# The second column pair of w_down's first half: eleven seven-product blocks laid between the second up stage's projections

## The chip, the cores and the metric

The kernel runs on one core of a Trainium2 chip. The metric is the device time of one execution in microseconds, and the profile is that of one execution. PE is the engine that multiplies matrices, DVE, ACT and POOL are the three engines that work on vectors, and SP issues the loads and stores. What PE writes goes to one of eight PSUM banks (128 partitions by 512 floats), and DVE or ACT reads it from there.

## The reference

One decoder layer in float32 on 256 positions with 2048 channels: an input projection, two kinds of attention, an output projection, and then the channel mixer, with which this change is concerned:

```python
h = rmsnorm(x, pre_ffn_g[l])
u = causal_dwconv(h @ w_up[l], conv_w[l], conv_b[l])          # 256 x 11264
gate, val = jnp.split(u, 2, axis=-1)
y = (jax.nn.gelu(gate, approximate=True) * val) @ w_down[l]   # 5632 -> 2048
x = x + rmsnorm(y, post_ffn_g[l])
```

## The kernel before

A float32 operand is split into a high and a low part (`fp32r`): ACT casts the high part, DVE subtracts it for the low part, and a product is then three matmuls (high by high, high by low, low by high). Each weight unit of 128x1024 therefore costs one load by SP, one cast on ACT and one subtraction on DVE before PE may use it. The loads go to a ring of five `raw` tiles, the parts to a ring of five `wpair` tiles.

The channel mixer runs in two halves of 2816 hidden channels. The **up stage** of a half has eleven steps `g`. A step projects 256 gate channels and then 256 value channels (`proj_S`: 96 matmuls of 128x256 into one PSUM bank, from four weight units). After each of the two, DVE reads the bank into a tile `u` (`rows_of`, below called the evacuation), ACT and DVE run the convolution on it, ACT applies the gelu to the gate channels, and DVE multiplies. The result is split into the tiles `G` (two per step), which are the stationary operands of the down stage. `LONG` and `LATE` are orders in which the high and low parts of the four units are used: `LONG` begins with the high part of the first unit, `LATE` with its low part.

The **down stage** of a half multiplies `G` by 22 blocks of rows of w_down, in two column pairs, `n = 0` and `n = 2` (each is two blocks of 512 columns). Two row blocks are handled together as a 2x2 block product. A *four* takes one column block the plain way, so a pair of columns costs 8 products; a *seven* does the pair with 7 products (Strassen's scheme in Winograd's form). One product is three matmuls of 128x512, so a seven has 21 where two fours have 24. A seven needs sums of `G` tiles (POOL adds them, ACT and DVE split them into `sums` or `more`) and sums of weight blocks. The weight sums are made on DVE when the block is used (four subtractions of 128x512, `L1105`), or were made earlier, in the up stage: `stage` loads a block into `staged`, subtracts on DVE (`L928`, four of 128x256, twice a block), and stores it to DRAM for later (`STORED`). `SEVENS` says how many sevens a column pair of a half has and after which pair of fours each stands. In half 0 both column pairs have six sevens and five pairs of fours. After the last seven `fold` adds four banks into `y_sb`, and `down` adds the others.

PE's order is the program's order. ACT's, DVE's, POOL's and SP's are set by a scheduler before the run; each engine then works strictly in its order, and an instruction that waits holds up everything behind it on its engine.

Of the kernel before, what the change touches and what calls it, by code (L numbers as in the profile page):

```python
# [17 lines left out]
P = 128  # L18
# [9 lines left out]
SEVENS = (((0, 0, 1, 1, 2, 2), (0, 0, 1, 1, 2, 2)), ((0, 0, 1, 1, 2), (0, 1, 2)))  # L28
STORED = (((0, 0, 1), (0, 0, 3), (0, 0, 5), (0, 2, 1), (0, 2, 3), (0, 2, 5), (1, 0, 1)), ((1, 0, 3), (1, 2, 0), (1, 2, 1), (1, 2, 2)))
# [5 lines left out]
def hybrid_layer(ctx: ExitStack, tc: tile.TileContext, x, pre_mix_g, w_in, b_forget, sinks,  # L35
# [817 lines left out]
    with tc.tile_pool(name="ffn", bufs=1) as fp:  # L853
# [123 lines left out]
        gbf = None  # L977
        for half in range(2):
            G = [fp.tile([P, 512], F32R, tag="G", bufs=FHALF, name=f"G{j}")[:, 0:512]
                 for j in range(FHALF)]  # L980
            most = max(len(at) for at in SEVENS[half])
            least = min(len(at) for at in SEVENS[half])
            sums = []

            def sums_at(u):
                w, at = 384 if u < least else 512, 768 * min(u, least) + 1024 * max(u - least, 0)
                if not u:
                    sums.append(main.tile([P, 4096], F32R, tag="x", name="sums"))
                if at + 2 * w <= 4096:
                    x = sums[0][:, at:at + 2 * w]  # L990
                else:
                    x = fp.tile([P, UNIT], F32R, tag="gb1", name="more")[:, 0:2 * w]
                sums.append((x[:, :w], x[:, w:]))
                return w, *sums[-1]

            for g in range(FHALF // 2):
                c0 = (half * (FHALF // 2) + g) * 256
                alt = (g + half) % 2
                if half == 0 and g == 0:
                    bg = first_gate()  # L1000
                    order.__exit__(None, None, None)
                    bv = [bank(), bank()]
                    proj_T(w_up, DFF + c0, bv, LONG)
                else:
                    bg = bank("att") if alt else bank()
                    proj_S(w_up, c0, bg, LATE if g + half == 1 else LONG)
                gates = []
                yy = fp.tile([P, 4, 256], F32, tag="yy", bufs=2, name="yy")
                for m, u in enumerate(rows_of(bg)):
# [7 lines left out]
                for m, u in enumerate(rows_of(bv)):  # L1017
# [3 lines left out]
                if g < most:  # L1021
# [6 lines left out]
                    if g < least:  # L1028
                        s1 = a21
# [4 lines left out]
                for m, y in enumerate(ys):  # L1034
                    gt = G[g * 2 + m]
                    split(gt[:, 0:256], gt[:, 256:512], y)
                if g < most:
                    w, *parts = sums_at(g)
                    split(*parts, s[:, :w])
                if not g:  # L1040
                    if half:
                        room = lambda: fp.tile([P, 4, 256], F32, tag="gb0", name="staged")
                    else:
                        four_of = main.tile([P, 4, 4, 256], F32, tag="y", name="staged")
                        rooms = [four_of[:, i] for i in range(4)]
                        room = lambda: rooms.append(rooms[0]) or rooms.pop(0)
# [10 lines left out]
            gains, downs = [], []  # L1057

            def down(t, n, b, gain=None):
                ys = y_sb[:, t, n * 512:(n + 1) * 512]  # L1060
                downs.append(dve.tensor_tensor(ys, b, ys, op=ALU.add))
                if half:
                    act.activation(junk, ys, AF.Square, scale=D ** -0.5,
                                   accum_out=ysq[t][:, n:n + 1])
                    (gain or pool.tensor_tensor)(
                        ys, ys, gbf[n // 2][:, n % 2 * 512:(n % 2 + 1) * 512], op=ALU.mult)

            LAST = FHALF // 2 - HOLD

            def products(b, held, hi, lo, opened, closes=False):  # L1070
                for i, (x, r) in enumerate(((held[0], hi), (held[0], lo), (held[1], hi))):
                    pe.matmul(b, x, r, start=b not in opened and not i,  # L1072
                              stop=closes and i == 2)
                opened.append(b)

            def parts_of(k, t):
                return G[k][:, t * P:(t + 1) * P], G[k][:, 256 + t * P:256 + (t + 1) * P]

            def split_into(dst, src, n):
                hi, lo = (x[:, :n * 512] for x in dst)  # L1080
                split(hi, lo, src[:, :n * 512])
                return [(hi[:, i:i + 512], lo[:, i:i + 512]) for i in range(0, n * 512, 512)]

            def seven(n, u, last, banks, opened):

                b, e, g, a, c, d, f = banks
                k = half * FHALF + u * 2
                t = in_dram.get((half, n, u))
                if t is None:
                    top, low = [w_load(w_rows(w_down, k + i, 1, n * 512, 1024), 1, 1024, raw=x)[0]  # L1090
                                for i, x in enumerate((None, fp.tile(
                                    [P, UNIT], F32, tag="yy", bufs=2, name="low")))]
                else:
                    top = w_load(w_rows(w_down, k, 1, n * 512, 512), 1, 512)[0]
                    low = w_load(w_rows(w_down, k + 1, 1, n * 512, 1024), 1, 1024)[0]
                s2, s3, s4, s1 = [
                    [x[:, i * P:i * P + P] for x in sums[1 + u]] if i < 3 or u >= least
                    else parts_of(u * 2, 1) for i in range(4)]
                (w11,) = split_into(w_parts(UNIT, held=False), top, 1)
                w21, w22 = split_into(w_parts(UNIT, held=False), low, 2)  # L1100
                if t is None:
                    b11, b12, b21, b22 = (x[:, i:i + 512] for x in (top, low) for i in (0, 512))
                    for y, p, q in ((b11, b12, b11), (b12, b22, b12), (b22, b22, b11),
                                    (b21, b21, b22)):
                        made = dve.tensor_tensor(y, p, q, op=ALU.subtract)  # L1105
                        if n and not u and y is b11:
                            tc.add_manual_dep(
                                made.ins, downs[-1].ins.name,
                                mybir.DependencyInfo(mybir.DependencyClass.NoSync,
# [203 lines left out]
```

## Time and profile before

| | us |
|---|---|
| median of 3 runs | 1053.0 (1052.75 to 1053.56) |
| the profiled execution: its own time | 1053.05 |
| the profiled execution: its span | 1051.2 |

Of the span PE is busy 99%, DVE 80%, ACT 60% and POOL 16%. The up stage of half 0 runs from 359.62 us (its second step) to 577.24, the down stage of half 0 to 688.80, the up stage of half 1 to 928.20, and the last down stage to the end. PE waits for nothing between 359 and 1046 us; it is the bound there. Where a table or a list below has a matmul group with 3 of its instructions missing, and a gap of that length, the records are missing and not the work.

### The profile page before, as it was taken

What the parts mean: (1) busy time and instruction counts of PE and PEld (TensorE: products, weight loads), DVE (VectorE), ACT (ScalarE), POOL (GpSimd) and SP (SyncE); (2) the same over time, 40 slices, a digit from 0 to 9 for tenths busy, and PEclk for the clock granted to TensorE, in tenths of its full rate; (3) what the DMA queues carried; (4) which work ended last, traced back from release to release, by engine and by line L of the source; (5) the groups of instructions that cost most, each with busy time, mean ns of one, the idle gap of its engine ahead of it and who ended that gap; (6) DMA issues with size and microseconds to landing.
All of it is one profiled execution on the core that took longest, in us unless ns stands there. A gap on an engine that the chain in (4) does not pass through costs nothing.

```text
span 1051.2 us, 19023 instructions
## 1 busy us (share of the span) xinstructions
PE 1040.2 (99%) x7240; PEld 958.1 (91%) x7240; DVE 836.9 (80%) x1364; ACT 627.7 (60%) x1026; POOL 168.0 (16%) x211
## 2 busy tenths in 40 slices
PE   9999999999999999999999999999999999999997
PEld 7899988888888999999999888899999999988886
DVE  5999877887477898888877988967788777789783
ACT  6777757667556755555555655645565555566561
POOL 3253245441122210100000000000111000000023
PEclk9999999999999999999999999999999999999998
DMA  8645556555874878988875886777677776767792
GB/s 292 199 128 169 182 157 213 164 179 172 292 252 148 257 253 289 290 271 268 285 233 168 263 270 222 241 238 239 222 228 249 227 241 221 235 210 257 243 320 104
DMA packets 187335, 238.98 MB, mean 227 GB/s; under 512 B 8268, under 2 KB 155116, under 8 KB 186348
## 3 DMA queue, kind: packets, MB, share of 16 engines
q1 hardware_dynamic: 186924, 237.30, 69.4%
q8 instruction: 57, 0.93, 0.3%
q10 hardware_dynamic: 320, 0.47, 0.1%
q14 instruction: 34, 0.28, 0.1%
HBM read 221.86 MB, written 15.75 MB: 226 GB/s over the span
## 4 chain that ended last, share of the span: by engine, by line
PE 90%; DVE 4%; ACT 2%; POOL 1%; DMA 1%; issue 1%; DVEq 0%; SPq 0%; ACTq 0%; POOLq 0%
PE bank_att L300 23%; PE bank_acc L300 21%; PE bank_acc L1072 15%; PE bank_acc L317 12%; PE bank_acc L263 5%; PE bank_att L1072 5%; PE bank_acc L270 3%; DVE wpair L122 1%; DMA raw<-in_w_in_dram 1%; PE bank_att L317 1%; POOL scr L450 1%; PE bank_att L518 1%; PE bank_att L483 1%; PE bank_att L527 1%; ACT p L501 1%
## 5 line engine op out<-in xcount | busy, mean ns | idle before, releaser
L122 DVE TENSOR_TENSOR wpair<-raw,wpair 128x1024 fp32r<-128x1024 f32 (+3 forms) x317 | 383.6, 1225 | 115.5 <-ACT wpair L119 114.5
L119 ACT CAST wpair<-raw 128x1024 fp32r<-128x1024 f32 (+3 forms) x316 | 320.4, 1032 | 153.5 <-issue 58.7
L300 PE MATMUL bank_att<-hT,wpair 128*128 128x256 f32 x2112 | 241.2, 276 | 0.0
L300 PEld LDWEIGHTS bank_att<-hT,wpair 128*128 128x128 f32 x2112 | 240.4, 188 | 0.2
L300 PE MATMUL bank_acc<-hT,wpair 128*128 128x256 f32 x1920 | 219.2, 276 | 0.0
L300 PEld LDWEIGHTS bank_acc<-hT,wpair 128*128 128x128 f32 x1920 | 218.3, 188 | 0.0
L1072 PE MATMUL bank_acc<-wpair,G 128*128 128x512 f32 x636 | 153.5, 389 | 0.0
L1072 PEld LDWEIGHTS bank_acc<-wpair,G 128*128 128x128 f32 x636 | 119.1, 188 | 24.5
L263 PE MATMUL bank_acc<-hT,wpair 128*128 128x512 f32 x384 | 94.9, 394 | 0.0
L263 PEld LDWEIGHTS bank_acc<-hT,wpair 128*128 128x128 f32 x384 | 69.5, 188 | 13.3
L317 PE MATMUL bank_acc<-wpair,oT 128*128 128x512 f32 x336 | 78.0, 391 | 0.0
L317 PEld LDWEIGHTS bank_acc<-wpair,oT 128*128 128x128 f32 x336 | 62.6, 188 | 12.8
L1030 POOL TENSOR_TENSOR s<-yy 128x128 f32<-128x128 f32 x11 | 7.5, 681 | 408.1 <-DVE yy L1019 408.1
L320 ACT CAST wpair<-raw 128x1024 fp32r<-128x1024 f32 (+1 forms) x54 | 48.0, 892 | 34.3 <-PE bank_acc L1072 17.2
L321 DVE TENSOR_TENSOR wpair<-raw,wpair 128x1024 fp32r<-128x1024 f32 (+1 forms) x54 | 54.8, 1023 | 13.6 <-ACT wpair L320 12.8
L899 ACT ACTIVATE yy<-u,cw 128x256 f32<-128x256 f32 x88 | 48.4, 596 | 20.8 <-DVE u L894 15.7
L270 PE MATMUL bank_acc<-hT,wpair 128*128 128x256 f32 x384 | 49.5, 281 | 0.0
L270 PEld LDWEIGHTS bank_acc<-hT,wpair 128*128 128x128 f32 x384 | 47.5, 188 | 1.4
L317 PE MATMUL bank_acc<-wpair,hT 128*128 128x384 f32 (+1 forms) x288 | 47.7, 321 | 0.0
L317 PEld LDWEIGHTS bank_acc<-wpair,hT 128*128 128x128 f32 x288 | 45.4, 188 | 0.1
L320 ACT CAST G<-yy 128x256 fp32r<-128x256 f32 x44 | 16.1, 406 | 47.5 <-POOL yy L1031 23.9
L901 DVE SCALAR_TENSOR_TENSOR yy<-u,cw,yy 128x256 f32<-128x256 f32 x88 | 39.1, 482 | 2.4 <-ACT yy L899 2.2
(255 smaller groups left out, 1207.1 us busy)
## 6 DMA issues: line engine op xcount, KB each, us to landing
raw<-in_w_up_dram SPq DMA_DIRECT2D x176, 512.0 KB, 4.6
raw<-in_w_down_dram SPq DMA_DIRECT2D x68, 512.0 KB, 5.1
raw<-in_w_in_dram SPq DMA_DIRECT2D x51, 512.0 KB, 5.3
raw<-in_w_out_dram SPq DMA_DIRECT2D x32, 512.0 KB, 4.7
staged<-in_w_down_dram SPq DMA_DIRECT2D x44, 256.0 KB, 5.4
t_dram<-staged SPq DMA_DIRECT2D x22, 512.0 KB, 3.2
raw<-t_dram SPq DMA_DIRECT2D x14, 512.0 KB, 3.8
raw<-in_w_in_dram SPq DMA_DIRECT2D x16, 384.0 KB, 3.2
```

Source lines behind the costliest of these rows:

```text
L119: i1 = act.copy(hi[:, cs], raw[:, cs])
L122: i2 = dve.tensor_tensor(lo[:, cs], raw[:, cs], hi[:, cs].bitcast(F32), op=ALU.subtract)
L263: pe.matmul(b, hi[:, a, m * P:(m + 1) * P], hT[:, kt, 0:512], start=(kt == 0), stop=(last == (0, kt)))
L270: pe.matmul(b[:, 256:512], lo[:, a, m * P:(m + 1) * P], hT[:, u * 4 + a, 0:256], start=False, stop=(last == (1, u * 4 + a)))
L300: pe.matmul(b[:, m * 256:(m + 1) * 256], ws[:, a, m * P:(m + 1) * P], hT[:, kt, i * 256:(i + 1) * 256], start=not begun, stop=last == (low ...
L317: pe.matmul(b, a, r[:, cols], start=(first and i == 0), stop=(last and i == 2))
L320: act.copy(hi, src)
L321: dve.tensor_tensor(lo, src, hi.bitcast(F32), op=ALU.subtract)
L450: pool.tensor_tensor(dst, dst, row, op=ALU.mult)
L899: act.activation(y, u[:, 2:258], AF.Identity, bias=cw[:, 3, ch:ch + 1], scale=cw[:, 2, ch:ch + 1])
L901: dve.scalar_tensor_tensor(y, u[:, 1:257], cw[:, 1, ch:ch + 1], y, op0=ALU.mult, op1=ALU.add)
L1072: pe.matmul(b, x, r, start=b not in opened and not i, stop=closes and i == 2)
```

## The change

It does five things.

1. `SEVENS[0][1]` becomes eleven sevens, and half 0's loop over `n` keeps `n = 0` alone. The column pair `n = 2` of half 0 is done in half 1's up stage: the first three products of `seven(g + 1)` stand after step `g`'s gate projection (`begin`), the other four after its value projection (`others.pop()()`). The first seven begins before step 0.
2. Its seven accumulators keep seven of the eight PSUM banks until step 9. All projections of half 1 go to the eighth (`alone`), but for the last value projection. They use `LATE`.
3. The sums of `G` for the sevens 6 to 10 are made in half 1 by a new function, `late_sums`, from the parts of `G`: eight additions on POOL (two of 128x256, six of 128x128), two casts and two splits.
4. These eleven sevens make their weight sums on DVE when they are used (`t is None`), with `low` in the single buffer `gb0`. `STORED` drops to eight blocks, all stored in half 0's up stage, with 8 ticks between loads in place of 10; half 1 stages none.
5. The tiles of `G` become two lists, and half 1's are allocated as half 0's are used up.

```diff
-SEVENS = (((0, 0, 1, 1, 2, 2), (0, 0, 1, 1, 2, 2)), ((0, 0, 1, 1, 2), (0, 1, 2)))
-STORED = (((0, 0, 1), (0, 0, 3), (0, 0, 5), (0, 2, 1), (0, 2, 3), (0, 2, 5), (1, 0, 1)), ((1, 0, 3), (1, 2, 0), (1, 2, 1), (1, 2, 2)))
+SEVENS = (((0, 0, 1, 1, 2, 2), (0,) * 11), ((0, 0, 1, 1, 2), (0, 1, 2)))
+STORED = ((0, 0, 1), (0, 0, 3), (0, 0, 5), (1, 0, 1), (1, 0, 3), (1, 2, 0), (1, 2, 1), (1, 2, 2))
+SUMS = (0, 768, 1536, 2304, None, 3328)
...
+        def late_sums(u):
+            s = fp.tile([P, 512], F32, tag="s", name="s")
+            s2, s3, s4, s1 = (s[:, i * P:i * P + P] for i in range(4))
+            d = fp.tile([P, 256], F32, tag="cs", bufs=1, name="cs")
...
+            pool.tensor_tensor(dv, x[:, :, 1, :], z[:, :, 1, :], op=ALU.add)
+            pool.tensor_tensor(s1, d[:, 0:P], d[:, P:256], op=ALU.add)
+            pool.tensor_tensor(dv, x[:, :, 0, :], x[:, :, 1, :], op=ALU.subtract)
+            pool.tensor_tensor(s3, d[:, 0:P], d[:, P:256], op=ALU.add)
+            pool.tensor_tensor(s2, s1, x[:, 0, 0, :], op=ALU.subtract)
+            pool.tensor_tensor(s2, s2, x[:, 1, 0, :], op=ALU.subtract)
+            pool.tensor_tensor(s4, z[:, 0, 0, :], s2, op=ALU.subtract)
+            pool.tensor_tensor(s4, s4, z[:, 1, 0, :], op=ALU.add)
+            w, hi, lo = sums_at(0, u)
+            split(hi, lo, s[:, :w])
+            split(*parts_of(0, u * 2, 1), s1)
...
-                                [P, UNIT], F32, tag="yy", bufs=2, name="low")))]
+                                [P, UNIT], F32, tag="gb0" if alone else "yy",
+                    bufs=1 if alone else 2, name="low")))]
...
         for half in range(2):
+            others = []
+            if half:
+                pair = [bank() for _ in range(3)] + [bank("att") for _ in range(4)]
+                alone, opened = bank(), []
+
+                def begin(u):
+                    others.append(seven(0, 2, u, u == FHALF // 2 - 1, pair, opened, True))
+
+                begin(0)
             for g in range(FHALF // 2):
...
-                    bg = bank("att") if alt else bank()
-                    proj_S(w_up, c0, bg, LATE if g + half == 1 else LONG)
+                    bg = alone if half else bank("att") if alt else bank()
+                    proj_S(w_up, c0, bg, LATE if half or g == 1 else LONG)
+                us = rows_of(bg)
+                if half and not g:
+                    others.pop()()
+                if half and g < FHALF // 2 - 1:
+                    begin(g + 1)
...
-                    bv = bank("att") if alt else bank()
-                    proj_S(w_up, DFF + c0, bv, LONG)
+                    bv = alone if half and g < FHALF // 2 - 1 else bank("att") if alt or half else bank()
+                    proj_S(w_up, DFF + c0, bv, LATE if half and g < FHALF // 2 - 1 else LONG)
+                us = rows_of(bv)
+                if others:
+                    others.pop()()
+                    if g == FHALF // 2 - 2:
+                        fold(0, 2, *(pair[i] for i in (3, 4, 5, 6)))
+                        for t, n, x in ((0, 2, 0), (1, 2, 2), (0, 3, 1)):
+                            down(0, t, n, pair[x])
+                    if g > 3 and g < FHALF // 2 - 2:
+                        late_sums(g + 2)
...
-                    for at in STORED[half]:
-                        start = stage(*at, start, 19 if half else 10, room)
+                    for at in STORED:
+                        start = stage(*at, start, 8,
+                                      lambda: rooms.append(rooms[0]) or rooms.pop(0))
...
-            for n in (0, 2):
+            for n in (0, 2) if half else (0,):
```

**PE, from the end of half 0's down stage into half 1's up stage.** In the rows an instruction has its line, what it writes and reads, and how often it follows itself; the lines of the changed kernel differ from those of the profile (products `L1072` becomes `L1040`, projections `L300` become `L301`). Before, `bank_att` and `bank_acc` change from step to step:

```order
L1072 MATMUL bank_acc<-wpair,G_3868 128x512 x6
L1072 MATMUL bank_acc<-wpair,G_3869 128x512 x6
L300 MATMUL bank_att<-hT_3542,wpair 128x256 x192
L300 MATMUL bank_acc<-hT_3542,wpair 128x256 x192
L300 MATMUL bank_att<-hT_3542,wpair 128x256 x192
```

And now, from step 2 of half 1 on:

```order
L301 MATMUL bank_acc<-hT_3542,wpair 128x256 x96
L1040 MATMUL bank_att<-wpair,G_3854 128x512 x3
L1040 MATMUL bank_acc<-wpair,G_3855 128x512 x3
L1040 MATMUL bank_acc<-wpair,sums 128x512 x3
L301 MATMUL bank_acc<-hT_3542,wpair 128x256 x96
L1040 MATMUL bank_att<-wpair,G_3854 128x512 x3
L1040 MATMUL bank_att<-wpair,sums 128x512 x6
L1040 MATMUL bank_acc<-wpair,G_3855 128x512 x3
```

Behind each projection of 96 matmuls now stand 9 or 12 matmuls of a seven, and then the next projection, which writes the same bank.

**DVE, half 1, step 3: from the multiplied value channels to the next gate evacuation.** `yy` holds the convolved channels, `wpair<-raw` (before `L122`, now `L123`) is the split of a projection's unit, and `u` is the evacuation. Before:

```order
L1019 TENSOR_TENSOR yy<-yy 128x256 x2
L321 TENSOR_TENSOR G_7770<-yy,G_7770 128x256
L321 TENSOR_TENSOR G_7771<-yy,G_7771 128x256
L122 TENSOR_TENSOR wpair<-raw,wpair 128x1024
L321 TENSOR_TENSOR sums<-s,sums 128x512
L122 TENSOR_TENSOR wpair<-raw,wpair 128x1024 x2
L894 TENSOR_TENSOR u_3838<-bank_att,rowf 128x2x256
```

And now, from the split of the sums on (`L1069` are the seven's four weight subtractions, which were `L1105`; the 128x128 split into `G` is `late_sums`'):

```order
L322 TENSOR_TENSOR sums<-s,sums 128x512
L322 TENSOR_TENSOR wpair<-raw,wpair 128x512
L322 TENSOR_TENSOR wpair<-low,wpair 128x1024
L1069 TENSOR_TENSOR raw<-raw 128x512
L322 TENSOR_TENSOR G_3860<-s,G_3860 128x128
L1069 TENSOR_TENSOR raw<-low,raw 128x512
L123 TENSOR_TENSOR wpair<-raw,wpair 128x1024
L1069 TENSOR_TENSOR low<-low,raw 128x512
L1069 TENSOR_TENSOR low<-low 128x512
L123 TENSOR_TENSOR wpair<-raw,wpair 128x1024
L895 TENSOR_TENSOR u_3838<-bank_acc,rowf 128x2x256
```

The evacuation now stands behind the next seven's splits and subtractions as well. Of the splits only two of a projection's four units stand ahead of it.

**POOL, half 1, step 3.** `L1183` to `L1186` are the sums of half 1's own sevens, which stand there before too (as `L1030` to `L1033`); the eight others are new.

```order
L1183 TENSOR_TENSOR s<-yy 128x128
L1184 TENSOR_TENSOR s<-yy 128x128
L1185 TENSOR_TENSOR s<-s,yy 128x128
L1186 TENSOR_TENSOR s<-yy,s 128x128
L1015 TENSOR_TENSOR s<-cs 128x128
L1016 TENSOR_TENSOR cs<-G_3860 128x256
L1018 TENSOR_TENSOR s<-s,G_3860 128x128
L1017 TENSOR_TENSOR s<-cs 128x128
L1019 TENSOR_TENSOR s<-s,G_3860 128x128
L1014 TENSOR_TENSOR cs<-G_3862,G_3863 128x256
L1020 TENSOR_TENSOR s<-G_3861,s 128x128
L1021 TENSOR_TENSOR s<-s,G_3861 128x128
```

POOL's order has five such groups of late sums (the last with seven instructions). The first follows step 3's own sums, the second step 4's, and the other three stand alone, in steps 5 to 7.

More of the change, by code (lines that the diff above doesn't have):

```diff
@@ L977, in hybrid_layer, with g_tile @@
         gbf = None
-        for half in range(2):
[L979 to L994, printed above, removed]
+        def g_tile(j):
+            return fp.tile([P, 512], F32R, tag="G", bufs=FHALF, name=f"G{j}")[:, 0:512]
@@ new lines, in hybrid_layer, with sums_at @@
+        G = [[g_tile(j) for j in range(FHALF)], []]
+        least = [min(len(at) for at in x) for x in SEVENS]
+        most = [len(x[0]) for x in SEVENS]
+        sums = []
+        def sums_at(half, u):
+            at, w = SUMS[min(u, 5)], 384 if u < least[half] or u > 5 else 512
+            if not sums:
+                sums.extend([main.tile([P, 4096], F32R, tag="x", name="sums"),
+                             fp.tile([P, UNIT], F32R, tag="gb1", name="more")])
+            x = sums[1][:, 0:2 * w] if at is None else sums[0][:, at:at + 2 * w]
+            return w, x[:, :w], x[:, w:]
@@ new lines, in products, with split_into @@
+        def products(b, held, hi, lo, opened, closes=False):
+            for i, (x, r) in enumerate(((held[0], hi), (held[0], lo), (held[1], hi))):
+                pe.matmul(b, x, r, start=b not in opened and not i,
+                          stop=closes and i == 2)
+            opened.append(b)
+        def split_into(dst, src, n):
+            hi, lo = (x[:, :n * 512] for x in dst)
+            split(hi, lo, src[:, :n * 512])
+            return [(hi[:, i:i + 512], lo[:, i:i + 512]) for i in range(0, n * 512, 512)]
@@ L1068, in hybrid_layer @@
[L1068 to L1091, printed above, removed]
-                                    [P, UNIT], F32, tag="yy", bufs=2, name="low")))]
[L1093 to L1109, printed above, removed]
-                                                     mybir.DependencyReason.DATA),
-                                reason="y first")
-                products(a, parts_of(u * 2, 0), *w11, opened, last)
-                products(b, parts_of(u * 2 + 1, 0), *w21, opened)
-                products(e, s4, *w22, opened)
-                def others():
-                    if t is None:
-                        one, two = top, low
-                    else:
-                        own = None if tail else fp.tile([P, UNIT], F32, tag="gb0", name="two")
-                        one, two = [w_load(t[:, i:i + 2, :], 2, 512, raw=x)[0]
-                                    for i, x in ((0, None), (2, own))]
-                    t1, t3 = split_into(w_parts(UNIT, held=False), one, 2)
-                    t4, t2 = split_into(w_parts(UNIT, held=False), two, 2)
-                    products(d, s1, *t1, opened, last)
-                    products(f, s3, *t3, opened, last)
-                    products(c, s2, *t2, opened, last)
-                    products(g, parts_of(u * 2 + 1, 1), *t4, opened)
-                return others
```

168 lines of the change are left out of this document (108 added, 60 removed).

## The prediction

> **What bounds the kernel now.** I read the table of busy times first, then the stretches by stage, then the chain of waits.
>
> ```profile
> PE 1040.2 (99%) x7240; PEld 958.1 (91%) x7240; DVE 836.9 (80%) x1364; ACT 627.7 (60%) x1026; POOL 168.0 (16%) x211
> ...
> 359.62:577.24 217.62, 217.62 (x1921) 217.62 (x1921) 181.31 (x287) 121.08 (x169) 17.75 (x26) 1.00 0.79 256
> 577.24:688.80 111.56, 111.56 (x495) 92.35 (x494) 99.89 (x113) 68.36 (x74) 0.00 (x0) 1.00 0.78 255
> 688.80:928.20 239.40, 239.40 (x2113) 239.40 (x2113) 183.13 (x275) 130.51 (x177) 13.29 (x20) 1.00 0.71 226
> ```
>
> The three lower rows are the up stage of half 0, its down stage, and the up stage of half 1; the columns are length, then busy time of PE, PE's weight loads, DVE, ACT and POOL, granted clock, DMA share, GB/s. PE has no gap in any of them at a full clock. So a matmul removed is time gained, and any wait put on PE is time lost. DVE is next: 83%, 90% and 76%. The change takes work out of the second stretch and puts it into the third.
>
> ```profile
> 577.94 6.81 PE bank_acc L1072 x30
> ...
> 775.86 21.76 PE bank_att L300 x192
> ```
>
> The chain gives the two prices on PE: a 128x512 product matmul takes 6.81 / 30 = 0.227 us, a projection matmul 21.76 / 192 = 0.113, so one projection (96) takes 10.88.
>
> **What the change removes.** In half 0's second column pair stood 6 sevens (126 matmuls) and 5 pairs of fours (120); now 11 sevens (231). 15 matmuls go: 15 x 0.227 = **3.4 us gained**, if PE never waits. Nothing else is taken from PE.
>
> **The new period.** A step of half 1 is now gate 10.88, 9 products 2.04, value 10.88, 12 products 2.72: 26.52 us. The gate's evacuation must be over before the value projection opens the same bank. Before, the other bank was open, and a late evacuation cost nothing. Whether PE waits is therefore decided by DVE's queue from one value evacuation to the end of the next gate evacuation. PE allows for it 2.72 + 10.88 + 2.04 = 15.64 us, less the lag with which the first evacuation starts:
>
> ```profile
> 785.13 2.36 DVE L122 TENSOR_TENSOR wpair<-raw,wpair 128x1024 fp32r<-128x1024 f32 x2 [0.26 <-ACT wpair L119]
> 787.41 0.68 DVE L894 TENSOR_TENSOR u<-bank_att,rowf 128x512 f32<-128x512 f32 x1
> 788.01 0.41 DVE L928 TENSOR_TENSOR staged<-staged 128x256 f32<-128x256 f32 x1
> 788.34 1.22 DVE L122 TENSOR_TENSOR wpair<-raw,wpair 128x1024 fp32r<-128x1024 f32 x1
> 789.47 0.88 DVE L901 SCALAR_TENSOR_TENSOR yy<-u,cw,yy 128x256 f32<-128x256 f32 x2
> 790.27 0.88 DVE L903 SCALAR_TENSOR_TENSOR yy<-u,cw,yy 128x256 f32<-128x256 f32 x2
> 791.06 1.34 DVE L928 TENSOR_TENSOR staged<-staged 128x256 f32<-128x256 f32 x3
> ```
>
> The gate that began at 775.86 ended at 786.74; its evacuation began at 787.41, 0.67 later. That leaves 15.64 - 0.67 = **15.0 us**. The rows also show that an instruction takes 0.08 less in the queue than its duration: two splits of 1.22 lie in 2.36, so 1.14 each; an evacuation 0.60, a convolution step 0.40.
>
> The queue's other pieces have rows in the stretches where they stand now (mean ns before the second bar):
>
> ```profile
> L321 DVE TENSOR_TENSOR wpair<-low,wpair 128x1024 fp32r<-128x1024 f32 x11 | 13.4, 1221 | 0.3
> L321 DVE TENSOR_TENSOR wpair<-raw,wpair 128x512 fp32r<-128x512 f32 x11 | 7.5, 685 | 0.0
> L1105 DVE TENSOR_TENSOR low<-low,raw 128x512 f32<-128x512 f32 x5 | 3.4, 686 | 0.0
> ...
> L321 DVE TENSOR_TENSOR G<-yy,G 128x256 fp32r<-128x256 f32 x20 | 9.0, 492 | 3.5 <-ACT G L320 2.7
> L1019 DVE TENSOR_TENSOR yy<-yy 128x256 f32<-128x256 f32 x20 | 7.5, 419 | 0.0
> L321 DVE TENSOR_TENSOR sums<-s,sums 128x384 fp32r<-128x384 f32 x3 | 1.7, 559 | 0.6 <-ACT sums L320 0.6
> ```
>
> In the order of the changed program: evacuation 0.60, split 1.14, four convolution steps 1.60, two multiplications 0.68, split 1.14, two `G` splits 0.82, the seven's splits 0.60 and 1.14, its subtractions 4 x 0.61 = 2.44, two splits 2.28, evacuation 0.68: **13.1 us**. Without POOL it fits, with 1.9 to spare. The other part of the period (gate evacuation to value evacuation: four splits, the convolution, two splits of the seven, about 9 us in 12.9) has room.
>
> **POOL's price.** POOL runs beside DVE in these stretches only where the sums are made:
>
> ```profile
> 737.05 0.84 POOL L1030 TENSOR_TENSOR s<-yy 128x128 f32<-128x128 f32 x1 [19.73 <-DVE yy L1019]
> 739.18 1.32 POOL L1033 TENSOR_TENSOR s<-yy,s 128x128 f32<-128x128 f32 x1
> 758.56 0.51 POOL L1030 TENSOR_TENSOR s<-yy 128x128 f32<-128x128 f32 x1 [18.06 <-DVE yy L1019]
> 760.23 0.59 POOL L1033 TENSOR_TENSOR s<-yy,s 128x128 f32<-128x128 f32 x1
> ...
> 737.16 1.62 DVE L928 TENSOR_TENSOR staged<-staged 128x256 f32<-128x256 f32 x3
> 738.71 1.48 DVE L122 TENSOR_TENSOR wpair<-raw,wpair 128x1024 fp32r<-128x1024 f32 x1
> ```
>
> Four sums take 760.82 - 758.56 = 2.26 us while DVE idles and 740.50 - 737.05 = 3.45 while it works, and DVE pays too: 1.48 for a split of 1.22, and 1.62 for three subtractions that take 1.34 at 791.06. So one 128x128 sum costs DVE between 0.14 (0.28 over two) and 0.26, and at the most what the last sum took beyond DVE's split (739.18 + 1.32 less 738.71 + 1.48: 0.31). The sum at 739.18 ended just after the split it ran into, so I read this as one of the two standing still, and take 0.26. A 128x256 sum has no clean row here; I count it as two. `late_sums` (six of the one, two of the other) is then ten: **2.6 us** on DVE (1.4 to 3.1).
>
> The Trainium skill's page "SBUF — State Buffer", section "Who interferes with whom", says that a DVE instruction with two SBUF inputs and a GpSimd instruction that reads SBUF take a shared port as an exclusive lock, for a whole instruction. The rows agree in kind, since splits, subtractions and `G` splits have two such inputs. By the page's letter a sum would cost DVE its own 0.51, twice what the row shows; that is the last rival below.
>
> Now step by step, waiting of PE in half 1's up stage:
>
> - **Steps 0 to 2** (own sums, 128x384). DVE's split of the sums waits for POOL: evacuation to multiplications 4.02, POOL 2.26 to 3.45, ACT's cast 0.51, the split 0.48, then the seven's part, two splits and the evacuation, 7.14: 14.4 to 15.6 against 15.0. I take 0.35 each: **1.1** (0 to 1.8).
> - **Step 3** has own sums of 128x512 (some 0.2 more in cast and split), a 128x128 split (0.2), and the first late sums behind its own, against the seven's subtractions: 15.0 + 0.4 + 2.6 = 18.0, **3.0** over (1.2 to 4.1).
> - **Step 4** also has the late split of 0.48, but the seven's two splits stand ahead of the sums and fill some 1 us of the wait: **2.5** (0.7 to 3.6).
> - **Steps 5 to 7**: 13.1, late splits 0.48 + 0.2, POOL 2.6: 16.4, 1.4 over. Some sums fall beside the convolution, before the splits, so I take 1.2 each: **3.6** (0 to 5.7). Steps 8 and 9 have no sums.
> - **The first value projection.** Seven 1's `low` can be loaded only when seven 0 has given up `gb0`, and the load takes 5.1:
>
> ```profile
> raw<-in_w_down_dram SPq DMA_DIRECT2D x68, 512.0 KB, 5.1
> ```
>
>   Behind it in DVE's queue stand the split (1.14, after a cast of 1.05), the gate's evacuation 0.60, a subtraction 0.61 and the value's first split 1.14. From seven 0's last split, some 6.5 after the gate's start, this ends at 6.5 + 5.1 + 1.05 + 1.14 + 0.60 + 0.61 + 1.14 = 16.1, against 15.64: **0.5** (0 to 1.6).
> - **Step 10's gate**: `fold` and `down` put seven additions of 0.60 (as `L1105`) between the last value evacuation and its last split: **0.6** (0 to 1).
>
> In **half 0** the staging goes from 6.4 to 8 subtractions in 16 ticks, and with 8 ticks they always fall in blocks of four ahead of a unit's split and an evacuation. Such a block takes 1.80:
>
> ```profile
> 467.05 1.80 DVE L928 TENSOR_TENSOR staged<-staged 128x256 f32<-128x256 f32 x4
> 468.76 1.22 DVE L122 TENSOR_TENSOR wpair<-raw,wpair 128x1024 fp32r<-128x1024 f32 x1
> 469.90 0.68 DVE L894 TENSOR_TENSOR u<-bank_att,rowf 128x512 f32<-128x512 f32 x1
> ```
>
> Value evacuation to gate evacuation: 4.02, POOL 2.26, cast and split of the sums 0.99, two splits 2.28, block 1.80, split 1.14: 12.5. Gate to value: 0.60 + 1.14 + 1.60, a wait of about 1.4 for ACT (the gelu and a cast), two splits 2.28, block 1.80, split 1.14: 10.0. The loop takes 22.5 for PE's 21.76; with 1.6 subtractions fewer (0.7) it just fitted. DVE slips 0.7 a step over the five steps with sums; two PSUM banks and the splits made ahead take the first of it. I take **2.0** (0 to 3.5). The DMA share there, 0.79, rises by a fourteenth at most; I cost that, and the waits it may add, at nothing beyond the bounds.
>
> The rest is hidden: casts (ACT 55% busy in that stage), the loads (half 1 stages nothing now), `LATE` (its low parts are split in advance).
>
> Sum: -3.4 + 1.1 + 3.0 + 2.5 + 3.6 + 0.5 + 0.6 + 2.0 = +9.9. On the profiled execution's 1053.05, which is the median to 0.05, that is **1063 us**. The forecast's own range is 1056 to 1069, since not all terms fall on one end.
>
> **The rivals.**
>
> *The gain arrives* (8%). If POOL costs DVE nothing when the two interleave, all of steps 5 to 9 fit (13.8 in 15.0), step 3 ends at 14.9, and the small terms may be zero: 1053.05 - 3.4 + up to 1 = 1050 to 1051. For it: the down stage ran DVE at 90% without one wait of PE. Against it: 1.48 for 1.22.
>
> *The stalls eat the gain* (17%). With 0.14 a sum, steps 0 to 2 cost 0, step 3 1.2, step 4 0.7, steps 5 to 7 0.2 each, the first and last 0.5 and 0.6, half 0 nothing: 3.6, so about 1053.3, within 1051 to 1055.
>
> *A full lock* (4%). Each sum costs DVE its own 0.5: ten are 5.0 in place of 2.6, five steps long: 12 more, 1075. Against it: the split at 738.71 paid half of that for the sum it met.
>
> *The sevens are not laid between the projections* (0%): PE's order shows them there.
>
> **How the numbers follow.** The forecast has 71%. A change of 0.2% (2.1 us) is about what a measurement of this kernel can tell from none. Faster is the first rival, 0.08; same the second, 0.17; slower the forecast and the lock, 0.75. The range 1053.5 to 1069.5 leaves out the first rival, part of the second, and the lock.
>
> **What would show it.** PE's waits, none now, would name DVE's `u` (`L895`) or the splits just behind it, once a step, largest at steps 3 and 4, smaller at 5 to 7, near nothing at 8 and 9. PE's product time would fall by 3.4. POOL's sums in steps 3 to 7 would take nearer 0.85 than 0.5, and DVE's splits beside them 1.4 or more. Half 0's up stage would be longer by about 2. I am wrong if PE runs steps 5 to 7 without a gap, or if its waits name loads or ACT's casts instead.

## The result, and the profile after

The changed kernel takes 1076.28 us (median of 4 runs, 1076.02 to 1076.67) against 1053.09 for the kernel before (4 runs): 1.022 times as long, 95% interval 1.0202 to 1.0238. It is slower by 23.2 us, where 9.9 were forecast, and outside the range that was given. The profiled execution took 1076.02; its span is 1074.2, 23.0 longer than before.

The table of busy times, and then the waits of PE from 345 to 1000 us (where it waited for nothing before); the columns of the second are what was waited for, then us in total, times, the longest:

```profile
PE 1047.9 (98%) x7225; PEld 960.8 (89%) x7225; DVE 866.9 (81%) x1391; ACT 632.5 (59%) x1046; POOL 206.3 (19%) x251
```

```profile
PE bank_acc L301 <- DVE u L895: 12.5, 8, 3.9
PE bank_acc L301 <- DVE wpair L123: 1.6, 4, 0.6
PE bank_att L301 <- DVE wpair L123: 0.8, 2, 0.4
```

Fifteen matmuls fewer are there, and PE is *busy* 7.7 us longer. So waiting is not all of it: PE also ran more slowly. The projections that follow a wait, in the timeline of PE (start, length, and in brackets the idle time before and what ended it), show both:

```profile
654.92 11.57 PE L301 MATMUL bank_acc<-hT,wpair 128*128 128x256 f32 x96 [0.19 <-DVE wpair L123]
669.08 11.07 PE L301 MATMUL bank_acc<-hT,wpair 128*128 128x256 f32 x96
682.76 11.19 PE L301 MATMUL bank_acc<-hT,wpair 128*128 128x256 f32 x96 [0.54 <-DVE u L895]
...
768.51 12.77 PE L301 MATMUL bank_acc<-hT,wpair 128*128 128x256 f32 x96 [3.87 <-DVE u L895]
800.85 14.07 PE L301 MATMUL bank_acc<-hT,wpair 128*128 128x256 f32 x96 [3.85 <-DVE u L895]
831.81 11.19 PE L301 MATMUL bank_acc<-hT,wpair 128*128 128x256 f32 x96 [1.17 <-DVE u L895]
...
935.02 4.82 PE L301 MATMUL bank_acc<-hT,wpair 128*128 128x256 f32 x40 [0.56 <-DVE wpair L123]
```

The first row is the value projection of step 0, the third that of step 1 (steps 2 and 3, with 0.59 each, step 7, with 1.20, and step 8, with 0.66, are left out), the next three are those of steps 4 to 6, and the last row is inside step 10's gate. The value projection of step `g + 1` waits for what DVE did after the value evacuation of step `g`. The second row is a projection without a wait: 11.07 (a group's end is modelled 0.16 past the next start, so a bracket of 0.54 costs PE 0.70). Behind a wait it takes 0.1 longer, but after the two long waits 1.7 and 3.0 longer. Three stretches of the same run, with the columns of the prediction's first fence (the granted clock stands before the DMA share):

```profile
764.64:768.51 3.87, 0.00 (x1) 0.00 (x1) 3.84 (x5) 0.68 (x2) 2.05 (x3) 1.00 0.45 135
768.51:772.00 3.49, 3.49 (x17) 3.49 (x18) 3.49 (x6) 2.06 (x4) 0.00 (x0) 0.56 0.73 222
800.85:805.00 4.15, 4.15 (x19) 4.15 (x20) 4.15 (x7) 2.43 (x4) 0.19 (x1) 0.50 0.75 218
```

After each of the two long waits the clock granted to PE was half for some microseconds. In the prediction nothing stands for that.

By stage, the up stage of half 0, and then half 0's down stage with half 1's up stage (first before, then after):

```profile
359.46:577.08 217.62, 217.62 (x1921) 217.62 (x1920) 181.31 (x287) 121.24 (x170) 17.75 (x26) 1.00 0.79 256
577.08:928.02 350.94, 350.94 (x2606) 331.73 (x2605) 283.04 (x386) 198.87 (x251) 13.29 (x20) 1.00 0.73 236
```

```profile
359.54:581.04 221.50, 219.82 (x1921) 218.38 (x1920) 184.60 (x295) 118.65 (x170) 16.92 (x27) 1.00 0.81 261
581.04:950.55 369.51, 356.31 (x2591) 333.83 (x2590) 308.37 (x404) 206.42 (x271) 52.28 (x59) 0.99 0.60 194
```

Half 0 lost 3.9, the interleaved stretch 18.6. The other 0.5 lies almost wholly behind them: from there to the end the kernel takes 123.65, and took 123.18.

### The profile page after: what moved, and what is told of

Read it like the earlier page. It is cut to its first block, busy times and chain, and to the rows that moved or that the text cites. A ratio compares the mean times of both kernels' runs of the same rounds, so it can differ in the third digit from the quotient of the medians.

```text
span 1074.2 us, 19038 instructions
## 1 busy us (share of the span) xinstructions
PE 1047.9 (98%) x7225; PEld 960.8 (89%) x7225; DVE 866.9 (81%) x1391; ACT 632.5 (59%) x1046; POOL 206.3 (19%) x251
## 4 chain that ended last, share of the span: by engine, by line
PE 64%; DVE 20%; issue 5%; ACT 4%; POOL 4%; DMA 2%; SPq 0%; DVEq 0%; ACTq 0%; POOLq 0%
PE bank_acc L301 17%; PE bank_acc L318 11%; PE bank_acc L1040 11%; DVE wpair L123 7%; PE bank_att L301 7%; PE bank_acc L264 5%; PE bank_att L1040 4%; PE bank_acc L271 3%; ACT wpair L120 2%; DVE wpair L322 2%; DVE u L895 1%; DVE yy L902 1%; POOL s L1183 1%; DVE yy L904 1%; PE bank_att L318 1%
## 5 line engine op out<-in xcount | busy, mean ns | idle before, releaser
L123 DVE TENSOR_TENSOR wpair<-raw,wpair 128x1024 fp32r<-128x1024 f32 (+3 forms) x307 | 373.2, 1230 | 103.7 <-ACT wpair L120 102.8
L120 ACT CAST wpair<-raw 128x1024 fp32r<-128x1024 f32 (+3 forms) x306 | 307.4, 1030 | 129.1 <-PE bank_acc L301 53.9
L301 PEld LDWEIGHTS bank_acc<-hT,wpair 128*128 128x128 f32 x2976 | 346.0, 190 | 19.8 <-DVE u L895 15.8
L301 PE MATMUL bank_acc<-hT,wpair 128*128 128x256 f32 x2976 | 349.4, 279 | 14.0 <-DVE u L895 12.5
L1040 PE MATMUL bank_acc<-wpair,G 128*128 128x512 f32 x546 | 134.6, 390 | 0.0
L301 PE MATMUL bank_att<-hT,wpair 128*128 128x256 f32 x1056 | 121.7, 277 | 0.8 <-DVE wpair L123 0.8
L301 PEld LDWEIGHTS bank_att<-hT,wpair 128*128 128x128 f32 x1056 | 120.6, 188 | 1.6 <-DVE wpair L123 1.2
L1040 PEld LDWEIGHTS bank_acc<-wpair,G 128*128 128x128 f32 x546 | 102.2, 188 | 21.5 <-DVE wpair L123 0.4
L1183 POOL TENSOR_TENSOR s<-yy 128x128 f32<-128x128 f32 x11 | 15.6, 1422 | 358.5 <-DVE yy L1172 358.5
L264 PEld LDWEIGHTS bank_acc<-hT,wpair 128*128 128x128 f32 x384 | 69.5, 188 | 13.3
L321 ACT CAST wpair<-low 128x1024 fp32r<-128x1024 f32 x34 | 35.7, 1050 | 26.9 <-DVE low L1069 9.6
L271 PE MATMUL bank_acc<-hT,wpair 128*128 128x256 f32 x384 | 49.5, 281 | 0.0
L271 PEld LDWEIGHTS bank_acc<-hT,wpair 128*128 128x128 f32 x384 | 47.4, 188 | 1.4
L322 DVE TENSOR_TENSOR wpair<-low,wpair 128x1024 fp32r<-128x1024 f32 x34 | 42.2, 1242 | 5.1 <-ACT wpair L321 4.9
```

Of the source, the lines that this page charges most:

```text
L120: i1 = act.copy(hi[:, cs], raw[:, cs])
L123: i2 = dve.tensor_tensor(lo[:, cs], raw[:, cs], hi[:, cs].bitcast(F32), op=ALU.subtract)
L264: pe.matmul(b, hi[:, a, m * P:(m + 1) * P], hT[:, kt, 0:512], start=(kt == 0), stop=(last == (0, kt)))
L271: pe.matmul(b[:, 256:512], lo[:, a, m * P:(m + 1) * P], hT[:, u * 4 + a, 0:256], start=False, stop=(last == (1, u * 4 + a)))
L301: pe.matmul(b[:, m * 256:(m + 1) * 256], ws[:, a, m * P:(m + 1) * P], hT[:, kt, i * 256:(i + 1) * 256], start=not begun, stop=last == (low ...
L321: act.copy(hi, src)
```

## The experiments

The theory after the result has four parts. POOL's additions and DVE hold each other up in the stretch from the value evacuation to the next gate evacuation, the late ones as forecast and the own ones more than forecast. A long wait then costs PE again at half clock. Half 0's loss comes from the spacing of the staged blocks. And two single waits, at the first value projection and in step 10's gate, have causes of their own. The main rival is that DVE's queue is too long by itself.

### The late additions left out

```diff
-            pool.tensor_tensor(dv, x[:, :, 1, :], z[:, :, 1, :], op=ALU.add)
...
-            pool.tensor_tensor(s4, s4, z[:, 1, 0, :], op=ALU.add)
+            pool.memset(s, 0.0)
```

> The eight POOL additions of late_sums are left out (one fill of their tile with zeros stands in their place, so the sevens 6 to 10 of half 0 get wrong sums); casts and splits stay. Theory: the waits of PE before the value projections of half 1 come from POOL's additions and DVE's instructions holding each other up in the stretch from the value evacuation to the next gate evacuation. Then the waits caused by steps 5 to 7 (1.3, 1.4 and 0.8, with 0.1 each for a slow start) vanish, those of steps 3 and 4 (4.0 each) fall to about 2, and PE's slow running behind them (1.6 and 2.9) goes or shrinks: 1064, at most 1067. Rival: DVE's queue is too long by itself (late splits, own sums of 128x512): steps 5 to 7 keep over 0.5 each, 3 and 4 over 3, and the time is 1072 or more.

Measured: 1066.28 (1064.68 to 1067.11), ratio to before 1.0126 (1.0111 to 1.0141). The waits caused by steps 5 to 7 are gone, those of steps 3 and 4 are 1.33 and 1.84, and both projections behind them take 11.19:

```profile
769.88 11.19 PE L301 MATMUL bank_acc<-hT,wpair 128*128 128x256 f32 x96 [1.33 <-DVE u L895]
798.64 11.19 PE L301 MATMUL bank_acc<-hT,wpair 128*128 128x256 f32 x96 [1.84 <-DVE u L895]
```

The interleaved stretch is 12.5 shorter than in the changed kernel (357.0, from PE's first product at 584.59 to 941.61). The theory gave 12.3. The whole time fell by 10.0 only, because half 0's up stage, which this edit does not touch, was longer in this execution; the last section takes that up. The rival falls.

DVE's queue, from a value evacuation's start to the next gate evacuation's end, gives the price of the additions. In the chain of waits of the changed kernel, the pairs for steps 3, 4 and 6 are:

```profile
749.40 0.68 DVE u L895
...
767.85 0.61 DVE u L895
...
781.77 0.69 DVE u L895
...
800.20 0.61 DVE u L895
...
843.49 0.69 DVE u L895
...
859.27 0.61 DVE u L895
```

That is 19.06, 19.04 and 16.39. Without the additions, in the timeline of DVE, for steps 3, 4 and 5:

```profile
753.32 0.68 DVE L895 TENSOR_TENSOR u<-bank_acc,rowf 128x512 f32<-128x512 f32 x1
769.14 0.68 DVE L895 TENSOR_TENSOR u<-bank_acc,rowf 128x512 f32<-128x512 f32 x1
781.57 0.68 DVE L895 TENSOR_TENSOR u<-bank_acc,rowf 128x512 f32<-128x512 f32 x1
797.90 0.68 DVE L895 TENSOR_TENSOR u<-bank_acc,rowf 128x512 f32<-128x512 f32 x1
810.32 0.68 DVE L895 TENSOR_TENSOR u<-bank_acc,rowf 128x512 f32<-128x512 f32 x1
823.99 0.68 DVE L895 TENSOR_TENSOR u<-bank_acc,rowf 128x512 f32<-128x512 f32 x1
```

16.50, 17.01 and 14.35. So the ten additions lengthen the queue by 2.6 in step 3 and by 2.0 in step 4. The 14.35 is no price of DVE's: there the two evacuations start 13.67 apart, which is PE's own pace (12 products and a projection, 13.66), and DVE stands idle for 0.44 in between. Read from the rows themselves, DVE's instructions of step 6 of the changed kernel are together 2.5 longer than the same ones of step 5 here. So the forecast's 2.6 was good, and for steps 5 to 7 its base of 13.8 too. For step 3 the base was not: without the additions it stood at 16.5, not 15.4.

### The late additions moved beside the gate's convolution

```diff
                     gates.append(y)
+                if half and g > 3 and g < FHALF // 2 - 2:
+                    added = late_sums(g + 2, gates[1])
...
                     if g > 3 and g < FHALF // 2 - 2:
-                        late_sums(g + 2)
+                        split_late(g + 2, *added)
```

`late_sums` now begins with a POOL copy of one column of `gates[1]` into `d`; `split_late` holds its two splits.

> The eight additions of late_sums are kept, but begin behind the gate's convolution of their step (a small POOL copy of one column of the gate ties them to it); their splits stay where they are. Theory: DVE has some 3 us to spare between the gate's and the value's evacuation, and none between the value's and the gate's, so the waits of steps 5 to 7 vanish, step 3's falls to 0.8, step 4's to 1.5, and the clock loss goes: 1062, within 1060 to 1065. Rival: the additions cost DVE the same wherever they stand and the wait only moves to the gate projections or to the splits: 1070 or more.

Measured: 1064.51 (1062.82 to 1065.72), ratio 1.011 (1.0095 to 1.0125). Steps 5 to 7 have no wait, step 3 leaves 1.25, step 4 still 2.27, where 0.8 and 1.5 were expected. There is no clock loss, and the gate projections got no new wait. So the same eight additions are almost free in the other half of the period. Most of step 4's wait is not theirs: without them it was 1.84. First POOL's row there, then DVE's:

```profile
782.18 4.45 POOL L1190 TENSOR_TENSOR s<-yy 128x128 f32<-128x128 f32 x1 [3.68 <-DVE yy L1179]
```

```profile
782.35 1.22 DVE L123 TENSOR_TENSOR wpair<-raw,wpair 128x1024 fp32r<-128x1024 f32 x1
783.49 0.42 DVE L1179 TENSOR_TENSOR yy<-yy 128x256 f32<-128x256 f32 x1
783.82 0.42 DVE L322 TENSOR_TENSOR G<-yy,G 128x256 fp32r<-128x256 f32 x1
784.15 0.69 DVE L322 TENSOR_TENSOR wpair<-raw,wpair 128x512 fp32r<-128x512 f32 x1
784.76 1.22 DVE L322 TENSOR_TENSOR wpair<-low,wpair 128x1024 fp32r<-128x1024 f32 x1
785.89 0.42 DVE L322 TENSOR_TENSOR G<-yy,G 128x256 fp32r<-128x256 f32 x1
788.82 0.69 DVE L322 TENSOR_TENSOR more<-s,more 128x512 fp32r<-128x512 f32 x1 [2.50 <-ACT more L321]
```

Step 4's own first addition, 0.46 to 0.51 long when nothing is in its way, took 4.45: it ended 0.32 after the last of six DVE instructions that follow each other without a gap, each at its undisturbed length. Then DVE itself stood 2.50 until POOL and ACT were done with the sums. The page "SBUF — State Buffer" of the Trainium skill, section "Who interferes with whom", lets the instruction that comes first hold the shared port for its whole length, and the other wait. Here POOL waited not for one instruction but for the train of six. That is not what always happens. In step 5 of the changed kernel POOL's late additions stand beside the same kinds of DVE instructions, which follow each other without a gap too, and there the two engines take turns: eight additions run in 6.5 us, and DVE's instructions are lengthened. Two of the rows:

```profile
820.58 1.48 DVE L123 TENSOR_TENSOR wpair<-raw,wpair 128x1024 fp32r<-128x1024 f32 x1
820.94 1.44 POOL L1019 TENSOR_TENSOR s<-s,G 128x128 f32<-128x128 f32 x1
```

Why the own first addition gets no turn and the late ones do is not shown by any run here.

### The own additions moved behind the next gate's convolution

In half 1 the additions, the splits of `G` and the split of the sums of step `g` become a function that is called in step `g + 1`; its first instruction on POOL is a copy of one column of `gates[0]`.

```diff
                     gates.append(y)
+                if waiting:
+                    waiting.pop()(gates[0])
```

> In half 1 a step's own additions, the splits of its G tiles and the split of its sums begin behind the gate's convolution of the next step (a small POOL copy of one column ties the first addition to it). late_sums and half 0 stay as they are. Theory: the waits of 0.7 to 0.8 caused by steps 0 to 2 are DVE standing behind POOL's additions (its split of the sums waits for them), and half of step 3's and 4's waits too, where POOL's first addition gets no turn while DVE's two-input instructions follow each other. Then steps 0 to 2 lose their waits, step 3's and 4's fall to 0.7 and 2.8, and with waits under 3 us the clock stays: 1065, within 1063 to 1068. Rival: DVE's work itself is too long there: steps 0 to 2 keep over 0.5 each, and 3 and 4 over 3: 1072 or more.

Measured: 1065.36 (1065.19 to 1069.07), ratio 1.0124 (1.011 to 1.0138). The time is as expected, the waits are not where they were expected. Those caused by steps 0 to 3 are gone (0.7 was expected of step 3), and step 4 leaves 0.3 (2.8 expected). In their place step 5 causes 2.52, where it caused 1.17: the second group of late sums now begins 4.6 us before step 5's value evacuation, in place of 22.1, and so its last additions and the whole third group stand behind that evacuation. That the time came out is in part luck.

DVE's queue in steps 0 to 2, evacuation to evacuation as above, fell from 15.8 to 14.3, which is PE's pace again (two evacuations 13.66 apart). The edit moves DVE's split of the sums too, so the fall alone doesn't part DVE's work from its waiting. The rows of the changed kernel do: in step 0, DVE stood 1.33 and 0.30 for ACT's casts of what POOL had added. Without these two, 15.8 is 14.2, and fits in 15.0.

Step 3 shows it more sharply. The small copy ties only the first addition; the other three don't depend on it, and POOL's order left them at their old place, right behind the value's multiplications. One of them took 7.26 there, beside ten DVE instructions without a gap, yet DVE ran at its undisturbed lengths and PE waited for nothing, because DVE's split of the sums now stood behind the gate's evacuation. So what made PE wait was DVE's standing still for POOL's result, not the place of the own additions.

The wait of 2.52 was again followed by a fall of the clock, which the expectation had ruled out under 3 us:

```profile
821.00:824.00 3.00, 3.00 (x16) 3.00 (x16) 2.83 (x6) 1.22 (x2) 0.00 (x0) 0.53 0.90 274
```

### PE kept busy through the two long waits

```diff
+                if half and g in (4, 5):
+                    for i in range(16):
+                        pe.matmul(pair[6], zero, hT[:, i, 0:512], start=False, stop=False)
                 if half or g:
                     bv = alone if half and g < FHALF // 2 - 1 else bank("att") if alt or half else bank()
```

> Sixteen matmuls of 128x512 with a stationary of zeros, added into a bank of the sevens, stand ahead of the value projections of steps 4 and 5 of half 1 (3.6 us each, where PE now waits 4.0). Theory: the granted clock falls to half because PE stood idle for about 4 us; kept busy, PE runs these two projections in 11.1 to 11.3 in place of 12.8 and 14.1, the clock stays at 1.00, and the time falls by 4.3 to 4.6, to 1072. Rival: PE is slow there because its operands come late, or the clock falls for another reason: the two projections keep their lengths, and the time is 1076 to 1077.

Measured: 1072.59 (1071.92 to 1073.49), ratio 1.0186 (1.0169 to 1.0203), 3.7 below the changed kernel. The two projections take 11.57 each and the clock stays at 1.00:

```profile
769.29:780.71 11.42, 11.42 (x97) 11.42 (x98) 7.96 (x10) 5.87 (x8) 0.00 (x0) 1.00 0.84 274
800.44:811.85 11.41, 11.41 (x97) 11.41 (x97) 8.14 (x10) 5.87 (x8) 0.20 (x1) 1.00 0.84 272
```

The operands came no earlier: DVE's queue behind the value evacuation was 19.1 both times, as in the changed kernel. PE only had something to do. So the slow running is the clock's, and the cause is PE's standing still. 11.57 in place of the expected 11.1 to 11.3 is the slower pace of which the last section tells.

### Blocks staged every 9 ticks

```diff
-                        start = stage(*at, start, 8,
+                        start = stage(*at, start, 9,
```

> The eight blocks staged in half 0's up stage are spaced by 9 ticks in place of 8. Theory: with 8 ticks four subtractions always stand ahead of the same split and DVE falls behind in the steps that also make sums; with 9 the blocks shift from projection to projection, half 0's up stage takes 217.8 in place of 221.5, and the time falls by 3.7, to 1072.6. Rival: the eighth block's DMA or the sums alone are the cause: the stage keeps over 220.5, and the time falls by less than 1.

Measured: 1071.86 (1071.6 to 1073.74), ratio 1.0185 (1.017 to 1.02). Half 0's up stage has the length that it had before, with the eighth block and its DMA in it:

```profile
359.59:577.21 217.62, 217.62 (x1921) 217.62 (x1920) 185.53 (x295) 121.37 (x170) 19.76 (x27) 1.00 0.82 266
```

So the eighth block's DMA is not the cause. DVE's rows fit the theory. With 8 ticks four subtractions stand together ahead of the last split and the evacuation, at every evacuation; with 9, one and three stand around a split here, and the place drifts from step to step:

```profile
440.84 1.80 DVE L929 TENSOR_TENSOR staged<-staged 128x256 f32<-128x256 f32 x4
442.56 1.22 DVE L123 TENSOR_TENSOR wpair<-raw,wpair 128x1024 fp32r<-128x1024 f32 x1
```

```profile
434.44 0.42 DVE L929 TENSOR_TENSOR staged<-staged 128x256 f32<-128x256 f32 x1
434.78 1.22 DVE L123 TENSOR_TENSOR wpair<-raw,wpair 128x1024 fp32r<-128x1024 f32 x1
435.92 1.34 DVE L929 TENSOR_TENSOR staged<-staged 128x256 f32<-128x256 f32 x3
```

At this evacuation it is four in both. With 9 ticks a step also has fewer of them, 7.1 on average for 8, so whether their place or their number a step counts was not tested apart.

### The two single waits

```diff
-                                [P, UNIT], F32, tag="gb0" if alone else "yy",
-                    bufs=1 if alone else 2, name="low")))]
+                                [P, UNIT], F32, tag="gb0" if alone and u else "yy",
+                    bufs=1 if alone and u else 2, name="low")))]
```

`fold` and the three `down` move from step 9, after the value evacuation, to step 10, after the gate evacuation.

> Two small places: the first laid seven has its low rows in a yy tile in place of gb0, so that the second's can be loaded at once; and fold with the three additions of down stands behind step 10's gate in place of step 9's value. Theory: the first value projection's wait (0.35, with 0.5 for a slow start) comes from the load that waits for gb0, and the wait of 0.7 inside step 10's gate from these seven additions: both vanish, 1074.7. Rival: both waits come from DVE's queue as it is in every step: nothing changes, 1076.

Measured: 1076.57 (1073.46 to 1078.91), ratio 1.022 (1.02 to 1.024). Both waits are gone from the trace: the first bracket of PE in half 1 is step 1's, and step 10's gate runs without one. The median did not fall by the 1.6: two of the four executions took 1078.6 and 1078.9, and the profiled one of them lost 3.6 in half 0 by the slower pace. The fastest run, 1073.46, is 2.8 under the changed kernel's median. Taken alone the times settle nothing; the pair below does.

### All of them, without and with the last

Blocks every 9 ticks, the late additions and the own additions moved as above, with (`comb2`) and without (`comb1`) the two single places.

> Three edits together: blocks staged every 9 ticks in half 0, the late additions behind the gate's convolution, and half 1's own additions and splits behind the next step's gate convolution. Theory (each term as it was measured alone): half 0's 3.9, the waits caused by steps 0 to 7 with the slow running behind them (2.5, 5.7, 7.0, 3.8) all go but for some 0.3; the first value projection's 0.85 and the gate's 0.7 in step 10 stay: 1053.6, within 1052.6 to 1055. Rival: additions from both sources now meet beside the gate's convolution in steps 4 and 5 and cost there what they cost before: 1057 or more.

> The same three edits with the two small places as well (the first seven's low rows in a yy tile, fold behind step 10's gate). Theory: no wait of PE is left, and of the 15 products saved (3.4) some 1.3 are lost again where PE goes from one matmul shape to the other (0.06 each time, 21 times): before less 2.0, so 1050.8, within 1050.2 to 1052.2. Rival: something else in the interleaved stage costs PE time that the waits do not show: as before or slower, 1053 or more.

Measured: 1052.82 (11 runs, 1051.69 to 1054.71), ratio 1.0 (0.9991 to 1.0009), and 1050.82 (11 runs, 1049.83 to 1051.37), ratio 0.9976 (0.9967 to 0.9984). The second beats both kernels: by 0.24% the kernel before, by 25.5 us the changed one. The two single places are worth 2.0, and the times of the two kernels don't overlap. PE waits for nothing in it from 345 to 1000 us; the interleaved stretch is

```profile
577.21:925.95 348.74, 348.74 (x2592) 329.47 (x2590) 301.37 (x406) 206.28 (x271) 64.85 (x70) 1.00 0.66 206
```

With no wait left, it is 2.2 shorter than before, not 3.4. The missing 1.2 lies where PE goes from one shape of matmul to the other, as three projections that follow each other in PE's timeline show:

```profile
850.88 11.07 PE L301 MATMUL bank_acc<-hT,wpair 128*128 128x256 f32 x96
...
863.86 11.07 PE L301 MATMUL bank_acc<-hT,wpair 128*128 128x256 f32 x96
...
877.52 2.68 PE L301 MATMUL bank_acc<-hT,wpair 128*128 128x256 f32 x22
```

A projection and nine products take 12.98 and a projection and twelve 13.66, where 10.88 + 2.04 = 12.92 and 10.88 + 2.72 = 13.60 were reckoned: 0.06 for each of some 21 such pairs. Whether it is the shape, or the change of bank and operands that goes with it, was not tried.

In steps 3 and 4 of this kernel, too, the tie holds only the first of the own additions. The next one took 7.26 and 5.53 there, and PE waited for neither.

## Why the prediction was wrong, point by point

The sign and the mechanism were right: PE waits for `u` (`L895`), largest at steps 3 and 4, smaller at 5 to 7, none at 8 and 9. The size was wrong by 13. By the prediction's own terms (a wait, and with a plus the slow running behind it):

| step of the prediction | forecast | measured |
|---|---|---|
| 15 matmuls fewer | -3.4 | -3.4, 1.2 of it lost again at the changes of shape (as read in the last run) |
| steps 0 to 2 | 1.1 | 2.2 + 0.3 |
| step 3 | 3.0 | 4.0 + 1.7 |
| step 4 | 2.5 | 4.0 + 3.0 |
| steps 5 to 7 | 3.6 | 3.5 + 0.4 |
| first value projection | 0.5 | 0.35 + 0.5 |
| step 10's gate | 0.6 | 0.7 |
| half 0 staging | 2.0 | 3.9 |

The measured terms sum to 22.4 of the 23.0. Of the remaining 0.6, 0.5 lies behind the interleaved stretch, where the forecast had no term; its cause was not sought.

- **What failed most is a term that was missing.** "PE's waits" were summed as if PE went on at full speed afterwards. Two waits of 4.0 cost 1.7 and 3.0 more at half clock, 4.5 more than the 0.1 each that a short wait costs. The run that kept PE busy got 3.7 of it back. The Trainium skill's page "TensorE: Matmul & The Clock Gate", section "Part 1: The HAM clock gate (the 'warmup' mystery)", says that the clock falls to half after an idle window of about 3.4 us; by it, the forecast's own upper bounds for steps 3 and 4 (4.1 and 3.6) called for this term. The trace agrees for the waits of 3.87 and 3.85; 2.52 was enough once (last section).
- **Steps 0 to 2, 3 and 4: the size of "evacuation to multiplications 4.02, POOL 2.26 to 3.45".** The queue was 15.76 in steps 0 to 2, where 14.4 to 15.6 was reckoned, and 16.5 and 17.0 in steps 3 and 4 without late additions, where 15.4 and 14.9 were. POOL's four own additions took 3.4 in steps 0 to 2, the upper end of the range, 3.8 in step 3 and 5.95 in step 4. The range was taken from before, where POOL's first addition took 0.51 and 0.84. Here it got no turn while DVE's instructions followed each other (1.65 in steps 0 to 2, 2.32 in step 3, 4.45 in step 4), and DVE then stood waiting for its result:

```profile
725.88 1.65 POOL L1183 TENSOR_TENSOR s<-yy 128x128 f32<-128x128 f32 x1 [24.08 <-DVE yy L1172]
...
753.37 2.32 POOL L1183 TENSOR_TENSOR s<-yy 128x128 f32<-128x128 f32 x1 [24.09 <-DVE yy L1172]
...
785.85 4.45 POOL L1183 TENSOR_TENSOR s<-yy 128x128 f32<-128x128 f32 x1 [19.08 <-DVE yy L1172]
```

  For step 4 the prediction let "the seven's two splits" fill the wait, and came out 0.5 under step 3. These two splits were among the six instructions for which POOL waited.
- **The late additions' 2.6** came out at 2.0 to 2.6, and steps 5 to 7 at 3.5 for 3.6. This term was right, and so was reading 1.48 for 1.22 as one of the two standing still.
- **A full lock** gave 1075, near the measured time, by another way. It asked for 5.0 for ten additions and some 2.4 more in each of steps 5 to 7; the queue there was 16.39, as forecast. The time alone would have spoken for it, the steps speak against it.
- **Half 0.** The cause was named rightly: undoing the spacing gave the 3.9 back. The forecast assumed that the slack before the first late step would absorb a part; in four steps PE's weight loads waited twice (0.6 for DVE's split, 0.2 for ACT's cast), and a step became 0.97 longer.
- **The two single waits** were placed rightly (both went with the edits made for them), and their sizes were near; the first had 0.5 more from the slow pace.
- **The gain** was whole on PE's count, but a change of shape costs some 0.06, which was reckoned at nothing.

## What to carry to other kernels

Price a wait of PE twice: once for itself, and above some 2.5 us again for the half clock behind it. Where one engine's result goes through POOL and back, don't take POOL's time from another place: in this kernel the same addition took 0.51, 0.84 or 4.45, by what DVE ran beside it. Lay the instruction that waits for the result into the half of the period in which the engine has time, and look in the order whether a tie holds every instruction that was meant. Work that the average has room for (DVE 81%) must still fit between the two events that bound it.

## What the runs showed of the hardware that was not expected

- **The clock falls after a wait well under 4 us, but not always.** It fell after waits of 3.87, 3.85 and 2.52, and did not after 2.27, 1.84 and 1.33. How long it stayed low varied for the same wait (1.7 and 3.0 lost in the changed kernel, 2.6 and 1.8 with blocks every 9 ticks). Nor is the time to the fall fixed. In the wait of 3.87 the clock stayed at 1.00 to its end; over the wait of 3.85 it was 0.84 on average, so it had fallen within it. If it goes straight from 1.00 to 0.50, that was some 2.6 into the wait (an estimate from the 0.84). What sets the moment was not tried.
- **POOL beside DVE's two-input instructions takes turns in one place and gets none in another.** One of the own additions waited for a train of six (4.45), another for a train of ten (7.26); the late additions of steps 5 to 7 took 0.52 to 1.44 each beside instructions of the same kinds. What decides is open.
- **A slower pace of PE at a full clock.** After a wait PE sometimes goes on at 0.118 for a 128x256 matmul in place of 0.113, and keeps that pace until the next change of shape. In half 0's up stage, where the shape does not change for 200 us, this cost 3.6 in the profiled executions without the late additions and with the two single places mended. The same 20 us of the changed kernel and of the one without late additions:

```profile
500.00:520.00 20.00, 20.00 (x179) 20.00 (x178) 17.65 (x30) 11.26 (x16) 0.74 (x1) 1.00 0.93 298
```

```profile
500.00:520.00 20.00, 20.00 (x172) 20.00 (x171) 17.66 (x30) 11.33 (x16) 0.00 (x0) 1.00 0.95 307
```

  172 matmuls for 179, nothing waits, and the clock is 1.00 in both. The row at 654.92 (11.57) is the same thing. It may be behind the spread of the kernels that still wait in half 0 (1062.8 to 1065.7, 1073.5 to 1078.9), but the changed kernel waits there too and spreads by 0.6 only. What sets the pace after a wait stays open.
